# A planner that assumes one transfer rate at the start and a lower one after, with a smaller margin behind weight blocks

## The chip, the cores and the metric

The kernel runs on one core of one Trainium2 chip. The metric is the device time of one launch in microseconds (us). Each time below is the median of several runs, or the time of the one profiled execution where this is said.

## The reference, cut to what matters

One decoder layer on 512 tokens of width 2048, in float32. All weights are read from the chip's memory once per launch.

```python
mod = silu(c) @ w_ada + b_ada                 # 2048 -> 6 x 2048: sh1, sc1, g1, sh2, sc2, g2
h   = rms_norm(x, norm1_g) * (1 + sc1) + sh1
u   = h @ w_in                                # 512 x 2048 @ 2048 x 5656, split in groups
y_conv = short_conv_mixer(u_b, u_c, u_h)      # 1024 channels
k_cmp  = compress(k, cmp_w1_k, cmp_w2_k)      # and v_cmp: a small MLP over blocks of 32 tokens
y_attn = nsa_attention(q, k_cmp, v_cmp, k_slc, v_slc, k_win, v_win, gates)   # 8 heads x 128
x   = x + g1 * (concat(norm(y_conv), norm(y_attn)) @ w_out)
h   = rms_norm(x, norm2_g) * (1 + sc2) + sh2
x   = x + g2 * (relu(h @ w_ff1) ** 2 @ w_ff2) # 2048 -> 8192 -> 2048
out = rms_norm(x, normf_g)
```

## The kernel before, in words

The program has three parts, one after the other: the projections (everything up to the last column of `u`, some 0 to 557 us), attention with the first half of `w_out` (to about 745 us), and the rest of `w_out` with the feed-forward network (to the end). Each part is first only recorded: an object of class `Order` takes down every instruction with its engine, an assumed cost, and what it depends on. `Order.emit` then plans the part several times (`passes`), keeps the shortest plan, and issues the instructions in the planned order. Each engine, and the queue of transfers on SyncE (SP), then runs its own list strictly in that order on the chip. What an instruction waits for is set by its data; what stands ahead of it on its engine is set by the plan.

In `Order.plan` a transfer is priced by `rate`: it takes the wire for size over rate, one transfer after another, and the next one may be planned no earlier than 2 us before the wire is free. 512 KB take 1.28 us at 410 GB/s and 1.54 us at 340 GB/s. Of all instructions that could go next, the one that can start earliest is taken; ties go to the one that is wanted first (`late`). `x.slack` is added to the moment from which a transfer may start: the loads of the modulation matrix wait `SLACK` us behind the moment when their buffer is free, so that a block of weights that becomes ready in that time is planned ahead of them.

What is loaded in the projections, all in pieces of 512 KB:

- 16 blocks each of `w_kv`, `w_cv`, 32 of `w_conv`, 16 of `w_q`, 8 of `w_v`, 16 of `cmp_w1` (the compress MLP). Each lands in one of three buffers `raw`. ScalarE (ACT) copies it to the high part, VectorE (DVE) subtracts that to get the low part (rows `wh<-raw`, and `sw<-raw` for `cmp_w1`), and TensorE (PE) multiplies. The subtraction frees the `raw` buffer. `wh` has two pairs, so ACT can copy a block only when PE is done with the block two before. A block of `w_kv`, `w_cv`, `w_conv`, `w_q` gives PE 24 matmuls of 512 columns, a block of `cmp_w1` only 12 of 256 columns.
- 192 pieces of `w_ada`, the modulation matrix, into a ring `wa` of eight buffers, later four. For each one DVE does one dot product (`t<-wa,cs`; the results go to `acc` or `late`), which frees the buffer. The first third (sh1, sc1) is needed for the tokens `h` and has no slack or a slack of its own; the rest (g1, sc2, sh2, g2) is needed only after the projections. These are the late modulation loads.

At the end of the projections SP loads the first blocks of `w_oc` (`w_out` for the convolution half), DVE finishes the last heads (`q`), the mixed rows (`mix`) and the last dot products, sums the modulation (`mod<-late`), and attention begins: PE computes scores `s<-kslc,q` into three score buffers, DVE turns each into `p` and `pc`, and only then can PE fill the buffer again. DVE's first attention instruction is the memset of `pc`. Between scores, PE has matmuls `pw<-mix,wh` of `w_oc` to do.

All instructions recorded through `Order` carry one line of the source in the profile (L123), so rows are told apart by their tiles.

Of the kernel before, what the change touches and what calls it, by code (L numbers as in the profile page):

```python
# [35 lines left out]
NMAIN = 29  # L36
NSIDE = 7
NWA = 8
NBANK = 6
SLACK = 4.0  # L40
SOON = 10.0
BEHIND = 11.0

# [6 lines left out]
class Order:  # L50
# [2 lines left out]

    class Node:
        __slots__ = ("i", "eng", "call", "cost", "lag", "size", "preds", "succs", "late", "loose", "born",
                     "begin", "ready", "left", "lane", "slack", "due")

    def __init__(self, tc, tag, count, passes=1, pace=0.000456, rate=340e3):  # L60
        self.tc, self.tag, self.count, self.passes = tc, tag, count, passes
        self.lane, self.kept, self.slack, self.wide, self.pace = 0, set(), 0.0, (0.11, 0.00182), pace
        self.rate = rate
        self.nodes, self.past, self.seen, self.rings = [], {}, {}, {}
        self.outer, self.loose, self.due = set(), False, 0.0
        for e in ("tensor", "vector", "scalar", "sync", "gpsimd"):
            setattr(self, e, Order.Engine(self, e, getattr(tc.nc, e)))
# [132 lines left out]
    def plan(self, ideal, t, fixed):  # L200
        nodes = self.nodes
        ends = {}
        for name, by in self.seen.items():
            for i in set(by):
                ends.setdefault(i, []).append(name)
        users = {name: len(set(v)) for name, v in self.seen.items()}
        mine = sorted((n for x in nodes for n in x.born), key=lambda n: int(n.rsplit("_", 1)[1]))
        rank = {n: k for k, n in enumerate(mine)}

        for x in reversed(nodes):  # L210
            move = x.cost + x.lag if not x.size else 2.5 + x.size / self.rate
            x.late = min([nodes[s].late - (move if nodes[s].eng != "tensor" or x.eng != "tensor" else x.cost)
                          for s in x.succs] + [ideal.get(x.i, t + 10.0 - x.due)])

        free = dict.fromkeys(("tensor", "vector", "scalar", "sync", "gpsimd"), 0.0)
        wire = 0.0
        ready = {e: [] for e in free}
        lanes = {}
        for i in fixed or [x.i for x in nodes if x.eng == "tensor" and not x.loose]:
            lanes.setdefault(0 if fixed else nodes[i].lane, []).append(i)  # L220
        for lane in lanes.values():
            lane.reverse()
        slots = sorted([0.0] * (self.count - len(self.outer)))
        given = []
        while slots and len(given) < len(mine):
            given.append(slots.pop(0))
        for x in nodes:
            x.left, x.ready = len(x.preds), 0.0
            if not x.left and (x.eng != "tensor" or x.loose):
                ready[x.eng].append(x)  # L230
        out = []
        while len(out) < len(nodes):
            best = None
            for e in free:
                c = [(x, 0, None) for x in ready[e]]
                if e == "tensor":
                    c = [(x, -1, None) for x in ready[e]]
                    c += [(nodes[q[-1]], k, q) for k, q in lanes.items() if q and not nodes[q[-1]].left]
                for x, k, q in c:
                    at = max(free[e], x.ready + x.slack, wire - 2.0 if x.size else 0.0)  # L240
                    if x.born:
                        last = max(rank[n] for n in x.born)
                        if last >= len(given):
                            continue
                        at = max(at, given[last])
                    key = (at, k, x.late, x.i)
                    if best is None or key < best[0]:
                        best = key, x, q
            (at, *_), x, q = best
            e = x.eng  # L250
            if q is not None:
                q.pop()
            else:
                ready[e].remove(x)
            x.begin = at
            free[e] = at + x.cost
            end = at + x.cost + x.lag
            if x.size:
                wire = max(wire, at + 1.5) + x.size / self.rate
                end = wire + 0.7  # L260
            for n in ends.get(x.i, ()):
                users[n] -= 1
                if not users[n] and (n in rank or n in self.outer) and n not in self.kept:
                    if len(given) < len(mine):
                        given.append(max([end] + given[-1:]))
            for s in x.succs:
                y = nodes[s]
                y.left -= 1
                y.ready = max(y.ready, free[e] if e == y.eng == "tensor" else end)
                if not y.left and (y.eng != "tensor" or y.loose):  # L270
                    ready[y.eng].append(y)
            out.append(x)
        return max(free.values()), out
# [3 lines left out]
def hybrid_layer(ctx: ExitStack, tc: tile.TileContext, a, out):  # L277
    nc = tc.nc
# [13 lines left out]
    def pair(dtype=F32, name="m"):  # L292
        return slot(dtype, name)[:, :2 * T].rearrange("p (a b) -> p a b", a=2)
# [22 lines left out]
        tc.keep_in_program_order(filler(nc.tensor))  # L316

    xs = [pair(name="x2") for _ in range(NK // 2)]
    nc = order = Order(tc, xs[0].tensor.tag, NMAIN, passes=6, pace=0.000444, rate=410e3)
    order.wide = (0.24, 0.0021)  # L320
    ts = [small.tile([P, T], F32, name="t", tag="t", bufs=5) for _ in range(5)]
    scr, temps = ts[0].bitcast(BF16), cycle(ts[1:])
# [18 lines left out]
    class lane:  # L341

        def __init__(self, n):
            self.n = n
# [95 lines left out]
    def ada_steps(n):  # L440

        acc = halves_of(n)
        for i in range(2):
            w = ring[turn[0] % (4 if 0 in part_done else NWA)]
            turn[0] += 1
            order.slack = SLACK if n // NK not in (M_SC1, M_SH1) else 0.0 if n % NK else BEHIND
            nc.sync.dma_start(out=w, in_=a["w_ada"][2 * n + i])
# [275 lines left out]
    def more_ada(n):  # L723
        for _ in range(min(n, len(todo))):
            m = todo.pop(0)
            acc = halves_of(m)
            for i in range(2):
                w = ring[turn[0] % 4]
                turn[0] += 1
                order.slack = SLACK  # L730
                nc.sync.dma_start(out=w, in_=a["w_ada"][2 * m + i])
# [235 lines left out]
    nc = tc.nc  # L967
    temps = cycle(ts)
    nc = order = Order(tc, mix[0].tensor.tag, NMAIN, passes=6)
# [148 lines left out]
    nc = order = Order(tc, x1[0].tensor.tag, NMAIN, pace=0.000444)  # L1118
# [530 lines left out]
```

## Time and profile before

| what | value |
|---|---|
| median of 3 runs (lowest to highest) | 2099.62 us (2099.16 to 2104.02) |
| the profiled execution: time, span | 2096.75 us, 2095.0 us |
| mean granted TensorE clock | 0.991 |
| busy share of the span: PE, DVE, ACT, POOL | 98%, 90%, 48%, 6% |
| read from memory, written to it | 383.53 MB, 68.16 MB |

The span is the time from the first to the last instruction; the execution's own time has 1.75 us around it. In the profile a matmul's end is modelled, so a PE that is shown busy can still run below its peak; a row in which PE sat idle, with what ended the idle time, is firmer. A wait is put down to the last of the things waited for. "Granted clock" is the share of TensorE's full clock that it was given.

### The profile page before, as it was taken

What the parts mean: (1) busy time and instruction counts of PE and PEld (TensorE: products, weight loads), DVE (VectorE), ACT (ScalarE), POOL (GpSimd) and SP (SyncE); (2) the same over time, 40 slices, a digit from 0 to 9 for tenths busy, and PEclk for the clock granted to TensorE, in tenths of its full rate; (3) what the DMA queues carried; (4) which work ended last, traced back from release to release, by engine and by line L of the source; (5) the groups of instructions that cost most, each with busy time, mean ns of one, the idle gap of its engine ahead of it and who ended that gap; (6) DMA issues with size and microseconds to landing.
All of it is one profiled execution on the core that took longest, in us unless ns stands there. A gap on an engine that the chain in (4) does not pass through costs nothing.

```text
span 2095.0 us, 38213 instructions
## 1 busy us (share of the span) xinstructions
PE 2054.9 (98%) x15038; PEld 1920.0 (92%) x15038; DVE 1885.9 (90%) x3104; ACT 1007.7 (48%) x1465; POOL 128.1 (6%) x244
## 2 busy tenths in 40 slices
PE   9999999999999999999999999999999999999997
PEld 7888787898788779999999999999999999999997
DVE  7999997887898657999999999999999999999998
ACT  4432333232465435776666666666443333333355
POOL 0000000000000001022211121222000000000000
PEclk8999999999999999999999999999999999999999
DMA  8986488888511134476766666668975466476452
GB/s 343 348 325 231 174 294 324 311 292 307 200 63 69 62 134 152 136 227 207 211 210 205 208 214 198 213 206 285 347 274 211 163 248 227 138 254 239 144 181 99
DMA packets 144276, 454.19 MB, mean 217 GB/s; under 512 B 15840, under 2 KB 20320, under 8 KB 144096
## 3 DMA queue, kind: packets, MB, share of 16 engines
q1 hardware_dynamic: 108960, 386.72, 52.7%
q0 software_dynamic: 34048, 63.98, 10.1%
q8 instruction: 118, 1.93, 0.4%
q10 hardware_dynamic: 1088, 1.05, 0.1%
q14 instruction: 62, 0.51, 0.1%
HBM read 383.53 MB, written 68.16 MB: 216 GB/s over the span
## 4 chain that ended last, share of the span: by engine, by line
PE 90%; DVE 4%; DMA 3%; ACT 1%; issue 1%; SPq 0%; DVEq 0%; ACTq 0%
PE pf L123 63%; PE ps L123 19%; PE pw L123 4%; PE pv L123 2%; PE s L123 2%; DMA wa<-in_w_ada 1%; PE pt L123 1%; DMA raw<-in_cmp_w 1%; DVE wh L123 1%; DVE t L123 1%; DMA raw<-in_w_conv 0%; DMA x<-in_xt 0%; DVE x L123 0%; ACT wh L123 0%; DVE vz L123 0%
## 5 line engine op out<-in xcount | busy, mean ns | idle before, releaser
L123 PE MATMUL pf<-tk,hl 128*128 128x256 f32 x10704 | 1218.7, 276 | 0.5 <-ACT t L123 0.5
L123 PEld LDWEIGHTS pf<-tk,hl 128*128 128x128 f32 x10704 | 1217.1, 188 | 0.8 <-ACT t L123 0.7
L123 ACT ACTIVATE hl<-rw 128x1024 fp32r<-128x1024 f32 x269 | 285.7, 1063 | 338.3 <-PE pf L123 291.0
L123 DVE TENSOR_TENSOR hl<-rw,hl 128x1024 fp32r<-128x1024 f32 (+2 forms) x351 | 336.4, 968 | 32.4 <-ACT hl L123 31.9
L123 ACT ACTIVATE hl<-sg 128x1024 fp32r<-128x1024 f32 x180 | 191.1, 1062 | 217.3 <-PE pf L123 170.0
L123 DVE SCALAR_TENSOR_TENSOR t<-wa,cs 128x1024 bf16<-128x1024 f32 x190 | 231.7, 1220 | 30.7 <-DMA wa<-in_w_ada 29.0
L123 PE MATMUL ps<-h_m,wh 128*128 128x512 f32 x1080 | 252.3, 390 | 0.9 <-DVE h_m L123 0.9
L123 PEld LDWEIGHTS ps<-h_m,wh 128*128 128x128 f32 x1080 | 201.1, 188 | 42.4 <-DVE h_m L123 1.3
L123 ACT ACTIVATE wh<-raw 128x1024 fp32r<-128x1024 f32 (+1 forms) x106 | 112.7, 1064 | 257.3 <-PE ps L123 214.8
L123 DVE TENSOR_TENSOR hl<-sg,hl 128x1024 fp32r<-128x1024 f32 (+2 forms) x193 | 188.2, 986 | 27.1 <-ACT hl L123 26.9
L123 PE MATMUL ps<-h,wh 128*128 128x512 f32 x840 | 198.9, 395 | 2.9 <-ACT h L123 2.9
L123 PEld LDWEIGHTS ps<-h,wh 128*128 128x128 f32 x840 | 159.5, 191 | 36.7 <-ACT h L123 3.5
L123 DVE TENSOR_TENSOR wh<-raw,wh 128x1024 fp32r<-128x1024 f32 (+1 forms) x106 | 129.7, 1224 | 21.8 <-ACT wh L123 21.1
L123 DVE TENSOR_TENSOR sg<-sg,rw 128x1024 f32<-128x1024 f32 x120 | 145.8, 1215 | 0.0
L123 DVE SCALAR_TENSOR_TENSOR x<-pf,mod,x 128x256 f32<-128x256 f32 (+1 forms) x280 | 130.0, 483 | 13.5 <-PE pf L123 11.6
L123 POOL DMA_DIRECT2D g<-gt x192 | 101.1, 532 | 424.3 <-ACT hl L123 185.7
L123 PE MATMUL pw<-mix,wh 128*128 128x512 f32 x384 | 110.7, 407 | 0.0
L123 ACT ACTIVATE t<-t 128x512 f32<-128x512 f32 (+3 forms) x131 | 74.8, 571 | 15.9 <-DVE t L123 13.8
L123 DVE TENSOR_TENSOR sg<-rw 128x1024 f32<-128x1024 f32 x60 | 73.1, 1219 | 7.9 <-DMA rw<-in_w_f 4.8
L123 PEld LDWEIGHTS pw<-mix,wh 128*128 128x128 f32 x384 | 69.2, 190 | 10.8 <-issue 0.5
L123 DVE TENSOR_TENSOR rw<-rw 128x1024 f32<-128x1024 f32 x60 | 72.9, 1215 | 0.0
L123 ACT ACTIVATE gt<-t 128x512 fp32r<-128x512 f32 x96 | 60.3, 629 | 18.1 <-DVE t L123 15.2
(217 smaller groups left out, 1775.6 us busy)
## 6 DMA issues: line engine op xcount, KB each, us to landing
rw<-in_w_f SPq DMA_DIRECT2D x263, 512.0 KB, 4.2
wa<-in_w_ada SPq DMA_DIRECT2D x192, 512.0 KB, 6.0
tk<-g SPq DMA_DIRECT2D x114, 512.0 KB, 6.6
g<-gt POOLq DMA_DIRECT2D x192, 256.0 KB, 5.3
raw<-in_w_conv SPq DMA_DIRECT2D x32, 512.0 KB, 4.0
x<-in_xt SPq DMA_DIRECT2D x16, 512.0 KB, 5.7
raw<-in_w_kv SPq DMA_DIRECT2D x16, 512.0 KB, 5.5
raw<-in_w_cv SPq DMA_DIRECT2D x16, 512.0 KB, 5.1
```

Source lines behind the costliest of these rows:

```text
L123: x.i, x.eng, x.call = len(self.nodes), eng, (lambda: real(*args, **kw))
```

## The change

The first part's planner no longer takes 410 GB/s throughout. It takes 410 GB/s for transfers that begin before 40 us of planned time, and 340 GB/s for all later ones, also where it works back from when data is wanted (`late`). The two other planners took 340 GB/s before and still do. `SLACK` goes from 4 us to 1 us.

```diff
-SLACK = 4.0
+SLACK = 1.0
...
 class Order:
+    RATE, RUSH = 340e3, 410e3
...
-    def __init__(self, tc, tag, count, passes=1, pace=0.000456, rate=340e3):
+    def __init__(self, tc, tag, count, passes=1, pace=0.000456, rush=0.0):
...
-        self.rate = rate
+        self.rush = rush
...
-            move = x.cost + x.lag if not x.size else 2.5 + x.size / self.rate
+            move = x.cost + x.lag if not x.size else 2.5 + x.size / Order.RATE
...
             if x.size:
-                wire = max(wire, at + 1.5) + x.size / self.rate
+                wire = max(wire, at + 1.5)
+                wire += x.size / (Order.RUSH if wire < self.rush else Order.RATE)
                 end = wire + 0.7
...
-    nc = order = Order(tc, xs[0].tensor.tag, NMAIN, passes=6, pace=0.000444, rate=410e3)
+    nc = order = Order(tc, xs[0].tensor.tag, NMAIN, passes=6, pace=0.000444, rush=40.0)
```

No instruction is added or removed; the lists are permuted, in the projections only. POOL's list is the same. On SP the list is the same up to the seventh block of weights, on PE everything up to the first compress matmul. Two source lines were added, so L123 is L125 in the changed kernel. Three places:

First, the end of the projections on DVE. `wh<-raw` are subtractions (the last one is that of the first `w_oc` block), `t,late<-wa,cs` dot products, `MEMSET pc` is the first instruction of attention. Before:

```order
L123 TENSOR_TENSOR wh<-raw,wh 128x1024
L123 SCALAR_TENSOR_TENSOR q<-t,q 128x512
L123 TENSOR_TENSOR mix<-y,mix 128x512 x5
L123 TENSOR_TENSOR wh<-raw,wh 128x1024
L123 TENSOR_TENSOR mix<-y,mix 128x512 x3
L123 SCALAR_TENSOR_TENSOR t,late<-wa,cs 128x1024 x2
L123 TENSOR_TENSOR wh<-raw,wh 128x1024
L123 SCALAR_TENSOR_TENSOR t,late<-wa,cs 128x1024 x5
L123 TENSOR_TENSOR mod<-late 128x16
L123 TENSOR_TENSOR mod<-mod,vec 128x16
L123 MEMSET pc 128x96 x2
```

The same place on DVE in the changed kernel:

```order
L125 TENSOR_TENSOR wh<-raw,wh 128x1024
L125 SCALAR_TENSOR_TENSOR q<-t,q 128x512
L125 TENSOR_TENSOR mix<-y,mix 128x512 x6
L125 TENSOR_TENSOR wh<-raw,wh 128x1024
L125 SCALAR_TENSOR_TENSOR t,late<-wa,cs 128x1024 x3
L125 TENSOR_TENSOR wh<-raw,wh 128x1024
L125 SCALAR_TENSOR_TENSOR t,late<-wa,cs 128x1024
L125 TENSOR_TENSOR mod<-late 128x16
L125 TENSOR_TENSOR mod<-mod,vec 128x16
L125 TENSOR_TENSOR wh<-raw,wh 128x1024
L125 MEMSET pc 128x96 x2
```

Seven dot products stood behind the last `mix` rows, five of them behind the last subtraction; now four stand there, and all of them ahead of the last subtraction.

Second, the same place in SP's list of transfers, before:

```order
L123 DMA raw<-in_w_q 128x1024
L123 DMA wa<-in_w_ada 128x1024 x3
L123 DMA raw<-in_w_q 128x1024
L123 DMA wa<-in_w_ada 128x1024 x2
L123 DMA raw<-in_w_q 128x1024
L123 DMA wa<-in_w_ada 128x1024 x2
L123 DMA raw<-in_w_q 128x1024
L123 DMA wa<-in_w_ada 128x1024 x2
L123 DMA raw<-in_w_oc 128x1024
L123 DMA wa<-in_w_ada 128x1024 x4
L123 DMA raw<-in_w_oc 128x1024 x2
```

SP in the changed kernel, from the same `w_q` block (the thirteenth) on:

```order
L125 DMA raw<-in_w_q 128x1024
L125 DMA wa<-in_w_ada 128x1024 x3
L125 DMA raw<-in_w_q 128x1024
L125 DMA wa<-in_w_ada 128x1024
L125 DMA raw<-in_w_q 128x1024 x2
L125 DMA raw<-in_w_oc 128x1024 x3
```

The last six modulation loads stood behind the last `w_q` block, four of them behind the first `w_oc` block; now all 192 are ahead of the last two `w_q` blocks.

Third, the compress blocks in SP's list, from the third block of `cmp_w1` to the sixth, before:

```order
L123 DMA raw<-in_cmp_w 128x1024
L123 DMA raw<-in_w_conv 128x1024
L123 DMA wa<-in_w_ada 128x1024 x2
L123 DMA raw<-in_w_conv 128x1024
L123 DMA wa<-in_w_ada 128x1024
L123 DMA raw<-in_cmp_w 128x1024
L123 DMA wa<-in_w_ada 128x1024 x2
L123 DMA raw<-in_cmp_w 128x1024
L123 DMA wa<-in_w_ada 128x1024 x3
L123 DMA raw<-in_cmp_w 128x1024
```

The same stretch of SP's list in the changed kernel:

```order
L125 DMA raw<-in_cmp_w 128x1024
L125 DMA raw<-in_w_conv 128x1024
L125 DMA wa<-in_w_ada 128x1024 x2
L125 DMA raw<-in_cmp_w 128x1024
L125 DMA raw<-in_w_conv 128x1024
L125 DMA wa<-in_w_ada 128x1024 x2
L125 DMA raw<-in_cmp_w 128x1024
L125 DMA wa<-in_w_ada 128x1024 x3
L125 DMA raw<-in_cmp_w 128x1024
```

Between these two ends stood eight `wa` and two `w_conv`; now seven `wa` and two `w_conv` stand there, and the `wa` sit in other gaps.

Two counts over the whole lists: between the subtraction of the first `w_v` block and that of the eleventh `w_q` block DVE had 42 dot products and has 47 now. Between the first and the sixteenth compress block SP had 73 transfers and has 74 now; of the sixteen, the ninth, thirteenth and fourteenth stand two, two and three transfers further back in SP's list while PE uses them at the same place in its list, five matmuls and eight matmuls earlier.

## The prediction, before the run

> **What bounds the kernel now.** I read the page first, then the stretches, then the waits of PE. Its top and the shares of the chain that ended last:
>
> ```profile
> span 2095.0 us, 38213 instructions
> PE 2054.9 (98%) x15038; PEld 1920.0 (92%) x15038; DVE 1885.9 (90%) x3104; ACT 1007.7 (48%) x1465; POOL 128.1 (6%) x244
> PE 90%; DVE 4%; DMA 3%; ACT 1%; issue 1%; SPq 0%; DVEq 0%; ACTq 0%
> ```
>
> PE is the bound; 10% of the chain is other engines. The change permutes the projections only, so only PE's idle time there, and what it causes, can be won. The busy time by stretch (columns: PE, its weight loads, DVE, ACT, POOL, granted clock, DMA share, GB/s):
>
> ```profile
> 0.00:45.00 45.00, 39.98 (x166) 30.99 (x167) 33.05 (x57) 20.79 (x28) 0.20 (x4) 0.81 0.96 376
> 45.00:205.00 160.00, 159.07 (x702) 131.44 (x701) 152.21 (x262) 58.59 (x72) 0.00 (x0) 1.00 0.82 299
> 205.00:375.00 170.00, 162.79 (x802) 133.57 (x801) 148.11 (x208) 61.45 (x71) 0.00 (x0) 1.00 0.73 265
> 375.00:540.00 165.00, 162.94 (x898) 142.21 (x897) 136.38 (x217) 44.78 (x65) 0.00 (x0) 1.00 0.85 299
> 540.00:558.00 18.00, 18.00 (x86) 15.07 (x85) 17.89 (x27) 9.39 (x15) 0.00 (x0) 1.00 0.36 124
> 558.00:564.00 6.00, 0.83 (x4) 0.39 (x3) 4.31 (x15) 0.34 (x2) 0.00 (x0) 0.70 1.01 387
> 564.00:571.00 7.00, 7.00 (x29) 6.52 (x30) 3.61 (x25) 4.13 (x17) 0.00 (x0) 0.52 0.24 97
> 571.00:735.00 164.00, 164.00 (x864) 133.01 (x864) 135.26 (x389) 90.11 (x227) 0.00 (x0) 1.00 0.21 68
> ```
>
> PE's idle time is 5.0 us at the start, 0.9 in 45 to 205, 7.2 in 205 to 375 (where the compress blocks come in), 2.1 in 375 to 540, and 5.2 in the six microseconds in which the projections give way to attention. There the clock also falls, to 0.52 over the next seven. Behind it, to 735, PE is shown busy throughout: what PE gains at 564 it keeps. The wire is full only at the start (376 GB/s) and at the seam (387); in between it carries 265 to 299. All waits of PE from 205 to the seam (total, times, longest):
>
> ```profile
> PE ps L123 <- ACT sw L123: 6.3, 7, 1.6
> PE ps L123 <- DVE vv L123: 1.4, 1, 1.4
> PE ps L123 <- DVE sw L123: 0.7, 1, 0.7
> PE ps L123 <- DVE t L123: 0.6, 1, 0.6
> ```
>
> Compress blocks (`sw`) make 7.0 of these 9.0 us. Ordinary blocks make none.
>
> **The seam, step by step.** PE, SP and DVE in order of time there:
>
> ```profile
> 556.74 1.13 PE L123 MATMUL s<-kslc,q 128*128 128x160 f32 x9
> 557.71 0.91 PE L123 MATMUL pw<-mix,wh 128*128 128x512 f32 x3
> 563.79 0.93 PE L123 MATMUL s<-kslc,q 128*128 128x160 f32 x3 [5.17 <-DVE pc L123]
> ...
> 570.87 0.38 PE L123 MATMUL s<-kslc,q 128*128 128x288 f32 x1
> 541.46 14.52 SPq L123 DMA_DIRECT2D wa<-in_w_ada  x4
> 553.26 1.22 DVE L123 TENSOR_TENSOR wh<-raw,wh 128x1024 fp32r<-128x1024 f32 x1
> 554.39 1.22 DVE L123 SCALAR_TENSOR_TENSOR t<-wa,cs 128x1024 bf16<-128x1024 f32 x1
> 561.01 1.22 DVE L123 SCALAR_TENSOR_TENSOR t<-wa,cs 128x1024 bf16<-128x1024 f32 x1 [1.59 <-DMA wa<-in_w_ada]
> 562.63 0.25 DVE L123 MEMSET pc<- 128x96 f32 x2
> ```
>
> PE fills three score buffers, does three `pw`, and then stands 5.17 us until DVE has read a score. DVE could not: behind its last subtraction (553.26) it had five dot products, the last of which waited 1.59 us for its load, then the sums; the memset of `pc` came at 562.63. The load was late because SP spent 14.52 us on the last four, each behind the dot product that frees its buffer of the ring.
>
> *Term 1, the wait.* In the new lists all loads of `w_ada` are issued ahead of the last two `w_q` blocks, and the memset of `pc` stands directly behind the last subtraction. That one's time is set by PE, which frees `wh`: 553.26 + 1.22 gives `pc` at about 554.5, eight microseconds earlier and two before PE's first score. Even if DVE came 3 us late it would be there before PE is done with its three `pw` (558.62). Between the last `mix` and `pc` DVE had seven dot products and one subtraction, and has four and three: 3 x 1.3 us less, 2 x 1.22 us more, and the subtractions keep PE's pace. The whole 5.2 us go. Ends: 0 (DVE late by more than 5 us) and -5.2. I take -5.2. What is late next is DVE's own work on each score, 0.28 us and two short reads, which the `pw` cover.
>
> *Term 2, the clock.*
>
> ```profile
> 560.00:561.00 1.00, 0.00 (x0) 0.00 (x0) 0.00 (x0) 0.00 (x0) 0.00 (x0) 0.71 0.99 389
> 570.00:571.00 1.00, 1.00 (x7) 1.00 (x7) 0.08 (x1) 0.00 (x0) 0.00 (x0) 0.67 0.00 0
> ```
>
> 0.71 of one microsecond puts the fall to half at 560.4, 1.8 us after PE went idle; 0.67 puts the return at 570.7, 6.9 us after it resumed. PE ran 563.8 to 570.7 at half clock: at most 6.9 / 2 = 3.45 us are lost, and nothing if DVE sets the pace there. DVE is busy 3.61 of 7 us, so it is mostly PE: I take -2.8, ends 0 and -3.45. [...]
>
> **The compress blocks.** One of the waits, from its cause on:
>
> ```profile
> 249.43 0.33 SPq L123 DMA_DIRECT2D raw<-in_cmp_w  x1
> 254.88 1.22 DVE L123 SCALAR_TENSOR_TENSOR t<-wa,cs 128x1024 bf16<-128x1024 f32 x1 [1.87 <-DMA wa<-in_w_ada]
> 256.11 1.06 ACT L123 ACTIVATE sw<-raw 128x1024 fp32r<-128x1024 f32 x1 [1.99 <-DMA raw<-in_cmp_w]
> 257.21 0.33 PE L123 MATMUL ps<-sw,chi 128*66 128x256 f32 x1 [1.48 <-ACT sw L123]
> ...
> raw<-in_cmp_w SPq DMA_DIRECT2D x16, 512.0 KB, 5.1
> wa<-in_w_ada SPq DMA_DIRECT2D x192, 512.0 KB, 6.0
> ```
>
> Issued at 249.43, landed at 256.1, copied, and PE had waited. From issue to landing these take a median of 5.1 and the loads 6.0 us; at 410 GB/s the plan counts 1.5 + 1.28 + 0.7 = 3.5 us for a lone one, at 340 it counts 3.7. Both are optimistic, the new one 0.3 us less so per transfer and more where they queue.
>
> *Term 3.* For a gain speaks that the wire carried 265 GB/s there, under the new rate. For a loss: three compress blocks stand two or three transfers further back while PE wants them no later. The stretch has 74 transfers where it had 73, so the total load is the same. Both kinds of change act on single blocks, in both directions. Ends: -7.0 (all of those waits gone) and +7.0 (as much again). I take 0, midway, since the nearest row, the sum of the waits, is bound to either side alike.
>
> **The rows ahead of 205 us and the other moved rows.** SP's list is the same up to the seventh weight block, and between 45 and 205 PE loses 0.9 us. What covers a permutation there is that ACT waits for PE, not for data:
>
> ```profile
> ACT wh L123 <- PE ps L123: 214.8, 60, 5.9
> ```
>
> An ordinary block sits in its buffer until PE frees a `wh`. I cost this at nothing. Cover gone, each block would cost PE what it comes late.
>
> *Term 4, more dot products per block later on.* From the first `w_v` to the eleventh `w_q` block (412 to 520 us) DVE has 47 dot products instead of 42, 5 x 1.3 = 6.5 us more. The stretch, and what DVE waited for in it:
>
> ```profile
> 412.00:520.00 108.00, 105.94 (x642) 95.19 (x641) 85.99 (x140) 29.76 (x44) 0.00 (x0) 1.00 0.85 300
> DVE t L123 <- DMA wa<-in_w_ada: 14.9, 13, 3.0
> DVE wh L123 <- ACT wh L123: 6.3, 7, 1.9
> ```
>
> 86.0 busy plus 21.2 of waits is 107.2 of 108 us. With 92.5 busy, 15.5 us are left for waits. If the waits stay at 21.2, DVE and the subtractions behind its waits come late by 21.2 - 15.5 = 5.7 us. But a DVE that runs later finds more loads landed, and the loads themselves stand earlier. A ring of four needs 6.0 + 1.3 + 0.4 (issue) = 7.7 us for four dot products, 1.9 each, where 108 / 47 = 2.3 us are to be had. Ends: 0 and +5.7. I take +1.0, nearer to the row of the ring, which does not bind.
>
> **Sum.** -5.2 - 2.8 + 0 + 1.0 = -7.0 us on the profiled execution's 2096.75, 2089.75. The median of the runs is 2099.62, 2.9 us above that execution; forecast 2099.62 - 7.0 = 2092.6, 0.33% faster. About 0.3%, 6.3 us, is what a measurement of this kernel can tell from no change, so this is a forecast near that line.
>
> **The rivals.**
>
> *Larger gain.* The plan, nearer to what the wire gives, also clears the compress waits, and term 4 is nothing: -5.2 - 2.8 - 7.0 = -15.0, 2084.6. For it: 265 and 299 GB/s measured against 340 planned. Against: the latency is still planned two microseconds short, and those blocks did not move forward in SP's list. [...]
>
> *No change.* The gain at the seam is paid back by DVE in the `w_v` and `w_q` blocks: term 4 at its end, +5.7, gives -2.3 and 2097.3. It comes about where the ring's waits do not shrink when DVE is fuller: 13 waits for `wa` there say that the ring is close. For it also: a change that fixes little else. Against: the ring's 1.9 us per dot product.
>
> *Slower.* One mechanism: compress blocks that come so late that PE idles over 1.8 us, and the clock halves in mid-stage. Two or three transfers at 524288 bytes / 299 GB/s = 1.75 us are 3.5 to 5.3 us; the ninth, thirteenth and fourteenth block are the candidates. Each such wait costs about 4 us and 3.45 at half clock, 7.5. One leaves a small gain, two give -7.0 + 15 = +8, 2107.6: it decides from the second on. Against it: SP there waits on buffers more than on bytes (DMA share 0.73), so places in the list cost less than a transfer each. [...]
>
> **How the numbers follow.** The likeliest case, seam repaired and the rest about even, gets 0.52, with a range of its own of 2088 to 2098 and so three fifths of it faster by over 0.3% (0.31) and the rest within (0.21). Larger gain 0.15, all faster. No change 0.19. Slower 0.14. That makes 0.46 faster, 0.40 the same, 0.14 slower. The range takes in the larger gain to its figure and the no-change case with the spread of the runs, and leaves out the slower case: 2084.5 to 2101.
>
> **What would show it.** Term 1: no idle row of PE over 1 us between the last `w_q` matmul and the twelfth score; the memset of `pc` within 1 us of the last subtraction. Term 2: a granted clock of 1.00 from 540 to 735. Term 3: the sum of PE's waits for `sw` between 0 and 14 us, and no dip of the clock. Term 4: PE's idle time in the `w_v` and `w_q` blocks under 3 us. The forecast is wrong if `pc` is still late (DVE behind by over 4 us at the last `wh`), or if a compress wait passes 1.8 us and halves the clock.

## The result, and the profile after

The changed kernel takes 2080.81 us (median of 5 runs, 2080.06 to 2082.51), the kernel before 2099.42 us on the same chip (5 runs, 2096.21 to 2104.02). The ratio is 0.9912, 95% interval 0.9898 to 0.9925: 0.88% faster, where 0.33% was forecast, and outside the range. The profiled executions, 2082.51 and 2096.75 us, lie 14.2 us apart, the medians 18.6. On another chip the unchanged files gave 2083.01 against 2097.69, 14.7 apart (e7 below).

The head of the page after, and its busy time by stretch, in the columns of the prediction:

```profile
span 2080.7 us, 38230 instructions
PE 2051.0 (99%) x15038; PEld 1917.6 (92%) x15038; DVE 1885.8 (91%) x3104; ACT 1007.1 (48%) x1465; POOL 128.4 (6%) x244
```

```profile
45.00:205.00 160.00, 160.00 (x706) 132.21 (x705) 152.74 (x264) 58.96 (x73) 0.00 (x0) 1.00 0.83 301
205.00:375.00 170.00, 165.65 (x816) 135.96 (x815) 151.88 (x216) 62.30 (x74) 0.00 (x0) 1.00 0.78 274
375.00:540.00 165.00, 164.38 (x905) 143.85 (x904) 147.74 (x233) 49.06 (x71) 0.00 (x0) 1.00 0.86 307
540.00:558.00 18.00, 18.00 (x99) 15.60 (x98) 11.51 (x46) 9.12 (x24) 0.00 (x0) 1.00 0.38 131
558.00:564.00 6.00, 6.00 (x34) 5.14 (x34) 5.61 (x26) 3.50 (x12) 0.00 (x0) 1.00 0.28 87
564.00:571.00 7.00, 7.00 (x42) 6.09 (x40) 6.54 (x22) 5.38 (x17) 0.00 (x0) 1.00 0.00 0
```

From 540 to 571 PE has no idle time, and its clock is 1.00. From 205 to 540 it idles 5.0 us instead of 9.3, and from 45 to 205 none instead of 0.9. PE's waits from 205 to 545 are now:

```profile
PE ps L125 <- DVE sw L125: 1.9, 3, 1.5
PE ps L125 <- ACT sw L125: 1.5, 4, 0.7
PE ps L125 <- DVE t L125: 0.8, 1, 0.8
PE ps L125 <- DVE vv L125: 0.5, 1, 0.5
```

Compress blocks make 3.4 us (7.0 before), all waits 4.7 (9.0). The handover to attention, in order of time:

```profile
542.74 1.22 DVE L125 SCALAR_TENSOR_TENSOR t<-wa,cs 128x1024 bf16<-128x1024 f32 x1
...
547.04 1.23 DVE L125 TENSOR_TENSOR wh<-raw,wh 128x1024 fp32r<-128x1024 f32 x1 [2.65 <-ACT wh L125]
548.23 0.25 DVE L125 MEMSET pc<- 128x96 f32 x2
...
551.41 1.13 PE L125 MATMUL s<-kslc,q 128*128 128x160 f32 x9
...
553.12 0.46 PE L125 MATMUL s<-kslc,q 128*128 128x160 f32 x3
```

The last dot product begins at 542.74, the memset of `pc` follows the last subtraction at 548.23, three microseconds ahead of the first score, and the second group of scores (553.12) waits for nothing.

Two distances tell where the time went. From PE's first score to the first matmul of the third part (first `pf`) the profile has 191.8 us before (556.74 to 748.56) and 183.2 after (551.41 to 734.62): -8.6. The first score itself comes 5.3 earlier. From the first `pf` to the end it is 1346.4 and 1346.1.

### The profile page after: what moved, and what is told of

It is laid out like the page before. It is cut to its first block, busy times and chain, and to the rows that moved or that the text cites. A ratio compares the mean times of both kernels' runs of the same rounds, so it can differ in the third digit from the quotient of the medians.

```text
span 2080.7 us, 38230 instructions
## 1 busy us (share of the span) xinstructions
PE 2051.0 (99%) x15038; PEld 1917.6 (92%) x15038; DVE 1885.8 (91%) x3104; ACT 1007.1 (48%) x1465; POOL 128.4 (6%) x244
## 4 chain that ended last, share of the span: by engine, by line
PE 91%; DVE 4%; DMA 3%; ACT 1%; issue 1%; SPq 0%; DVEq 0%; ACTq 0%
PE pf L125 64%; PE ps L125 19%; PE pw L125 4%; PE pv L125 2%; PE s L125 2%; PE pt L125 1%; DMA raw<-in_cmp_w 1%; DMA wa<-in_w_ada 1%; DVE wh L125 1%; DMA raw<-in_w_conv 1%; DVE t L125 1%; DMA x<-in_xt 0%; ACT wh L125 0%; DVE x L125 0%; DVE vz L125 0%
## 5 line engine op out<-in xcount | busy, mean ns | idle before, releaser
L125 PE MATMUL pf<-tk,hl 128*128 128x256 f32 x10704 | 1218.7, 276 | 0.5 <-ACT t L125 0.5
L125 PEld LDWEIGHTS pf<-tk,hl 128*128 128x128 f32 x10704 | 1217.1, 188 | 0.8 <-ACT t L125 0.7
L125 ACT ACTIVATE hl<-rw 128x1024 fp32r<-128x1024 f32 x269 | 285.6, 1063 | 339.0 <-PE pf L125 285.3
L125 DVE TENSOR_TENSOR hl<-rw,hl 128x1024 fp32r<-128x1024 f32 (+2 forms) x351 | 336.3, 967 | 32.4 <-ACT hl L125 32.0
L125 ACT ACTIVATE hl<-sg 128x1024 fp32r<-128x1024 f32 x180 | 191.1, 1062 | 219.5 <-PE pf L125 165.4
L125 PE MATMUL ps<-h_m,wh 128*128 128x512 f32 x1080 | 252.1, 390 | 0.0
L125 DVE SCALAR_TENSOR_TENSOR t<-wa,cs 128x1024 bf16<-128x1024 f32 x190 | 231.6, 1219 | 14.0 <-DMA wa<-in_w_ada 12.2
L125 PEld LDWEIGHTS ps<-h_m,wh 128*128 128x128 f32 x1080 | 201.0, 188 | 41.6 <-DVE h_m L125 0.4
L125 ACT ACTIVATE wh<-raw 128x1024 fp32r<-128x1024 f32 (+1 forms) x106 | 112.8, 1064 | 255.5 <-PE ps L125 226.7
L125 DVE TENSOR_TENSOR hl<-sg,hl 128x1024 fp32r<-128x1024 f32 (+2 forms) x193 | 188.2, 985 | 25.1 <-ACT hl L125 24.9
L125 PE MATMUL ps<-h,wh 128*128 128x512 f32 x840 | 198.8, 394 | 2.9 <-ACT h L125 2.9
L125 PEld LDWEIGHTS ps<-h,wh 128*128 128x128 f32 x840 | 159.0, 190 | 36.7 <-ACT h L125 3.5
L125 DVE TENSOR_TENSOR wh<-raw,wh 128x1024 fp32r<-128x1024 f32 (+1 forms) x106 | 129.8, 1225 | 23.3 <-ACT wh L125 22.6
L125 DVE TENSOR_TENSOR sg<-sg,rw 128x1024 f32<-128x1024 f32 x120 | 145.8, 1215 | 0.0
L125 DVE SCALAR_TENSOR_TENSOR x<-pf,mod,x 128x256 f32<-128x256 f32 (+1 forms) x280 | 129.8, 484 | 13.7 <-PE pf L125 11.8
L125 POOL DMA_DIRECT2D g<-gt x192 | 101.4, 533 | 425.0 <-issue 188.0
L125 PE MATMUL pw<-mix,wh 128*128 128x512 f32 x384 | 109.4, 404 | 0.0
L125 ACT ACTIVATE t<-t 128x512 f32<-128x512 f32 (+3 forms) x131 | 74.7, 571 | 15.6 <-DVE t L125 13.6
L125 DVE TENSOR_TENSOR sg<-rw 128x1024 f32<-128x1024 f32 x60 | 73.1, 1218 | 8.4 <-DMA rw<-in_w_f 6.0
L125 PEld LDWEIGHTS pw<-mix,wh 128*128 128x128 f32 x384 | 68.5, 189 | 10.7 <-issue 0.5
L125 DVE TENSOR_TENSOR rw<-rw 128x1024 f32<-128x1024 f32 x60 | 72.8, 1214 | 0.0
L125 ACT ACTIVATE gt<-t 128x512 fp32r<-128x512 f32 x96 | 60.2, 629 | 15.7 <-DVE t L125 13.4
```

The source lines that it names most:

```text
L125: x.i, x.eng, x.call = len(self.nodes), eng, (lambda: real(*args, **kw))
```

## The experiments

Sixteen experiments were run, e1 to e16 (e7 is the changed kernel once more). The table gives them in the words used below: the ratio to the kernel before on the same chip; the wait of PE at the handover ("seam"); the distance from first score to first `pf`; all waits of PE from 205 to 545; and of these the ones at compress blocks (`sw`). The medians are of 4 to 12 runs; the last four columns are each from one profiled execution of that kernel.

| kernel | median | ratio (95% interval) | seam wait | score to `pf` | waits 205 to 545 | of these at compress blocks |
|---|---|---|---|---|---|---|
| before | 2099.42 | 1 | 5.2 | 191.8 | 9.0 | 7.0 |
| changed | 2080.81 | 0.9912 (0.9898 to 0.9925) | none | 183.2 | 4.7 | 3.4 |
| e1, rate alone | 2098.16 | 1.0001 (0.9990 to 1.0012) | 11.0 | 198.1 | 3.7 | 3.2 |
| e2, margin alone | 2086.40 | 0.9949 (0.9936 to 0.9963) | none | 183.5 | 4.0 | 2.4 |
| e3, 340 from the start | 2083.22 | 0.9931 (0.9917 to 0.9945) | none | 183.2 | 3.5 | 2.7 |
| e4, before with PE kept busy | 2095.71 | 0.9987 (0.9976 to 0.9997) | 1.8 | 185.7 | 11.7 | 7.8 |
| e5, before, margin 7 | 2129.45 | 1.0144 (1.0126 to 1.0163) | 29.6 | 216.3 | 13.6 | 12.0 |
| e6, before, 375 GB/s | 2099.73 | 1.0008 (0.9998 to 1.0019) | 8.1 | 193.5 | 5.7 | 4.1 |
| e7, changed again | 2083.01 | 0.9929 (0.9917 to 0.9942) | none | 183.3 | 3.1 | 1.5 |
| e8, later landing | 2087.57 | 0.9947 (0.9935 to 0.9959) | none | 183.2 | 7.5 | 4.5 |
| e9, changed, 300 GB/s | 2106.73 | 1.0043 (1.0030 to 1.0056) | 9.5 | 204.6 | 4.2 | 1.1 |
| e10, changed, margin 0 | 2083.70 | 0.9928 (0.9916 to 0.9941) | none | 183.1 | 3.1 | 1.8 |
| e11, changed, margin 2 | 2084.76 | 0.9934 (0.9921 to 0.9946) | none | 183.2 | 4.4 | 2.8 |
| e12, one matmul ahead of the feed-forward | 2085.09 | 0.9934 (0.9920 to 0.9947) | none | 183.2 | 4.1 | 2.2 |
| e13, before, 12 loads uncoupled | 2099.32 | 0.9996 (0.9985 to 1.0008) | 4.4 | 191.7 | 8.5 | 6.5 |
| e14, changed, 12 loads uncoupled | 2082.06 | 0.9915 (0.9902 to 0.9927) | none | 183.2 | 3.4 | 2.4 |
| e15, before, loads uncoupled | 2092.64 | 0.9969 (0.9959 to 0.9979) | 2.8 | 191.3 | 5.4 | 4.9 |
| e16, changed, loads uncoupled | 2081.30 | 0.9913 (0.9899 to 0.9928) | none | 183.2 | 3.3 | 2.0 |

### Which half does it: e1, e2, e3, e7

e1 is the changed kernel with the old margin, e2 the kernel before with the new one, e3 the changed kernel without the first 40 us at 410 GB/s, e7 the changed kernel once more.

```diff
# e1, to the changed kernel
-SLACK = 1.0
+SLACK = 4.0
# e2, to the kernel before
-SLACK = 4.0
+SLACK = 1.0
# e3, to the changed kernel
-pace=0.000444, rush=40.0)
+pace=0.000444, rush=0.0)
```

> The changed kernel with SLACK back at 4 us, so the two rates alone. In its lists ten modulation loads stand behind the last w_q block, eight of them behind the first w_oc block, and seven dot products behind the last subtraction (before: six, four and five). Theory A (the rates ease the waits for compress blocks, the margin repairs the seam): the projections end some 4 us earlier than before (552 to 553 us), but PE's wait at the seam grows from 5.2 to 8 to 12 us and the clock halves again, so the time is 2099 to 2104 us, not faster than before. Theory B (the margin eases both): the projections end at 556 to 558 us, the seam is as bad as under A, time 2102 to 2108 us. Theory C (the rates do all of it): no wait at the seam, time near 2081 us.

> The kernel before with SLACK at 1 us, so the smaller margin alone, at 410 GB/s throughout. In its lists no modulation load stands behind the last seven w_q blocks and no dot product behind the last mix rows. Theory A: no wait of PE over 1 us at the seam and a granted clock of 1.00 there, -8 to -9 us; waits for compress blocks as before (6 to 8 us) or larger, because loads go ahead of compress blocks; projections end at 556 to 559 us; time 2090 to 2093 us. Theory B: projections end at 551 to 552 us, time 2081 to 2085 us. Theory C: the seam as before, time 2097 to 2101 us.

> The changed kernel with 340 GB/s from the first transfer on (rush=0). The seam's lists are like the changed kernel's, so no wait there under any theory. If the 410 GB/s of the first 40 us matter, PE idles more before 45 us (changed kernel: 5.5 us) and the time is 1 to 5 us above the changed kernel's 2080.8; if not, it is within 1.5 us of it (2079 to 2082.5).

> The changed kernel once more, for a second profile and for runs on one chip with the others. If its gain of 18.6 us over the kernel before holds where the profiles differ by 14.3 us, it comes out at 2079 to 2082 us beside a kernel before at 2098 to 2100; if part of the gain was chance between runs, at 2082 to 2086.

The margin alone gives 0.51% and repairs the seam whole (183.5). Its time, 2086.40, lies between the ranges of theories A and B: the seam came as A says, but the waits in 205 to 545 fell to 4.0 us, where A left them at 6 to 8. The rate alone gives nothing: it takes the waits in 205 to 545 down to 3.7 us, the first score comes at 548.33, 8.4 us earlier than before, and the seam gives it back:

```profile
563.09 0.93 PE L125 MATMUL s<-kslc,q 128*128 128x160 f32 x3 [11.02 <-DVE pc L125]
```

Scores begin at 548.33, and the second group waits 11.02 us for `pc`, which still stands behind the dot products. So the waits in the projections fall with either half, and the falls do not add (3.7 and 4.0 us alone, 4.7 and 3.1 together). The smaller margin is what repairs the seam; the lower rate alone made it worse. e3 and e7 differ by 0.2 us: the first 40 us at 410 GB/s made no difference that these runs tell. e7's time is in the range that its expectation left to chance between runs, so the gain is 15 to 19 us by these two comparisons. e7 also shows what a profile's detail varies by: 3.1 us of waits in 205 to 545 where the first run had 4.7. With the lists of before, three profiles have 9.0, 8.5 (e13) and 11.7 (e4).

### How much of each: e5, e6, e9, e10, e11

The same two numbers, moved past their values in both directions:

```diff
# e5, to the kernel before
-SLACK = 4.0
+SLACK = 7.0
# e6, to the kernel before
-passes=6, pace=0.000444, rate=410e3)
+passes=6, pace=0.000444, rate=375e3)
# e9, to the changed kernel: 300 GB/s in place of 340, in the first planner alone
+        self.rate = 300e3 if rush else Order.RATE
...
-                wire += x.size / (Order.RUSH if wire < self.rush else Order.RATE)
+                wire += x.size / (Order.RUSH if wire < self.rush else self.rate)
# e10 and e11, to the changed kernel
-SLACK = 1.0
+SLACK = 0.0   # e11: 2.0
```

> The kernel before with SLACK at 7 us instead of 4, still 410 GB/s: the margin alone, in the other direction. In its lists 18 dot products stand behind the last subtraction (before: five) and ten modulation loads behind the last w_q block. If the margin sets how far the late loads fall behind, and so the wait at the seam: 18 dot products at 1.3 us (data there) to 1.9 us (ring of four) from 554.4 us put pc at 578 to 588 us, so PE waits 19 to 30 us there instead of 5.2, and the time is 2112 to 2124 us. PE's waits between 205 us and the seam (before: 9.0 us): if the margin sets them too they grow to 10 us or more; if they differ from plan to plan without order they may come out anywhere from 3 to 10 us.

> The kernel before at 375 GB/s throughout, midway between its 410 and the changed kernel's 340, with SLACK still 4 us. Seven dot products and six loads behind the last subtraction and block, so the wait at the seam is 9 to 12 us as in the run with the rates alone (11.0), under any theory. Theory P (the slower the plan takes transfers to be, the fewer waits): PE's waits between 205 us and the seam lie between the 9.0 us of before and the 3.7 us of the rates alone, 5 to 8 us, DVE's waits for loads between 27 and 16 us; time 2098 to 2102 us. Theory L (the waits differ from plan to plan without order, and the plan before was a poor draw): they come out near 4 us or at 9 us and more.

> The changed kernel with 300 GB/s in place of 340 for the later part of the first plan; everything else as changed. Theory R (the lower rate itself brings the loads earlier to the dot products and so takes the matmuls' waits away; the seam only hears the margin): waits of the matmuls in 205-545 at or under the changed kernel's 3 to 5 us, the seam without a wait as at 340 GB/s with margin 1, time 2079 to 2084. Theory O (what counts is where the written-out order leaves the last loads and dot products, whichever number moved them): at 300 GB/s six wa loads stand behind the first w_oc block again and six dot products behind the last subtraction, so the wait before the first score returns with 8 to 11 us (rate alone, with as many loads behind, gave 11.0), the clock is halved there for 10 to 14 us, and the stretch from the first score's beginning to the FFN's first matmul takes 196 to 199 us in place of 183.2: 2091 to 2098.

> The changed kernel with the margin at 0 us in place of 1. All wa loads stand ahead of the last three w_q blocks. Theory M (a smaller margin is better until the weight blocks come too late): seam clean, 183.2 us from first score to FFN as with margin 1, and the matmuls' waits in 205-545 at 3 to 5 us: 2080 to 2084. Rival (loads let in ahead of blocks now make blocks land late): waits of matmuls or ScalarE for blocks grow to 7 us or more, 2086 to 2090.

> The changed kernel with the margin at 2 us in place of 1. Two wa loads stand behind the first w_oc block. If the seam's wait grows evenly with the margin (at 410 GB/s: 1 none, 4 5.2 us, 7 29.6 us), 0 to 2 us of it come back, under the 1.8 us of idleness after which the clock was halved before: 183 to 185.5 us from first score to FFN, time 2081 to 2086. If it is a step (the first load behind the w_oc block brings it), the wait is 4 us or more with half the clock for 10 us, 190 us to the FFN, and 2088 to 2092.

At margin 7 the wait at the seam is 29.57 us, in the expected range; the time, 2129.45, is above its range, since the projections too became longer (first score at 562.96, 6.2 us later than before). Its row for the scores, and its largest row of waits in 205 to 545:

```profile
595.68 0.93 PE L123 MATMUL s<-kslc,q 128*128 128x160 f32 x3 [29.57 <-DVE pc L123]
```

```profile
PE ps L123 <- ACT sw L123: 11.7, 9, 3.3
```

Margins of 0, 1 and 2 in the changed kernel all leave the seam clean, and their times lie within 4 us. At margin 2 two loads do stand behind the first `w_oc` block again, but their dot products stay ahead of the last subtraction. What decides is how many dot products stand between the last subtraction and `pc`: with none the seam has no wait; five make 5.2 us (before), six 9.5 (e9), seven 8.1 and 11.0 (e6, e1; in e1 PE began its first score 2.0 us ahead of the last subtraction, in e6 2.4 us behind it), eighteen 29.6 (e5). Margin 3 was not run, so where between 2 and 4 the wait comes in is open.

The rate alone, at margin 4, moves both places, in opposite directions: at 410, 375 and 340 GB/s (before, e6, e1) the waits in 205 to 545 are 9.0, 5.7 and 3.7 us, as theory P has it, and the wait at the seam is 5.2, 8.1 and 11.0 us. The times are the same within their intervals.

e9 is the sharpest miss of a simple story. A lower rate still, closer to what the wire carried in the trace before (265 to 299 GB/s), is slower than the kernel before (1.0043). Theory O named the place; the size it gave was too small (196 to 199 us from first score to `pf`, where it took 204.6, and half clock for 10 to 14 us, where it lasted 23.9), as PE also waited for ACT and for the last subtraction there. The seam of e9, PE and DVE apart:

```profile
558.40 1.22 PE L126 MATMUL pw<-mix,wh 128*128 128x512 f32 x2 [2.46 <-ACT qr L126]
561.24 0.80 PE L126 MATMUL pw<-mix,wh 128*128 128x512 f32 x1 [1.61 <-DVE wh L126]
571.55 0.93 PE L126 MATMUL s<-kslc,q 128*128 128x160 f32 x3 [9.52 <-DVE pc L126]
```

```profile
561.11 1.21 DVE L126 SCALAR_TENSOR_TENSOR t<-wa,cs 128x1024 bf16<-128x1024 f32 x1
...
568.78 1.23 DVE L126 SCALAR_TENSOR_TENSOR t<-wa,cs 128x1024 bf16<-128x1024 f32 x1 [0.29 <-DMA wa<-in_w_ada]
...
570.40 0.25 DVE L126 MEMSET pc<- 128x96 f32 x2
```

Six dot products, from 561.11 to 570.0, stand behind the last subtraction, of 1.2 us each and only 1.42 us of waits for loads. The waits in 205 to 545 are as small as in the changed kernel (4.2). A planned rate nearer to the measured one therefore does not by itself make the plan better; it moves loads, and where the last of them falls is decided by the whole plan.

### The clock at the handovers: e4, e12

e4 is the kernel before with five matmuls of no use ahead of the first score; e12 the changed kernel with one between attention and feed-forward. Their results are not read.

```diff
# e4; e12 has one, ahead of the first matmul of the feed-forward part
+    for _ in range(5):
+        tc.keep_in_program_order(tc.nc.tensor.matmul(turned[0], ones,
+            ones[:, None, :].to_broadcast([P, NQ, P]), start=True, stop=True))
```

> The kernel before with five extra matmuls (128x128 by 128x512 float32, about 0.86 us each at full clock) put on PE between the projections and the first score; their result is overwritten, nothing else moves. They fill most of the wait at the seam without shortening it: PE still cannot go on before DVE reaches pc at 562.6 us. If the half clock behind the wait costs what the prediction took (2.8 us, at most 3.45), the granted clock stays at 1.00 there and the time falls by 2 to 3.5 us to 2096 to 2097.5, although PE has 4.3 us more to do. If attention there is paced by DVE and ACT, or the extra matmuls only push the scores back, the time stays at 2099 to 2100 or rises by up to 1 us.

> The changed kernel with one matmul of no use (f32, 128x512, about 0.86 us at full clock) between attention and FFN, its result left unread in a buffer of PSUM. If the 3.4 us of half clock that some runs show there (731.9-735.3 in one, 747.9-751.3 in another) come from TensorE standing idle at this place, the stretch is at full clock and the kernel is up to 1.5 us faster, 2079 to 2083; if the idleness is elsewhere or chance, the matmul costs its own 0 to 0.9 us: 2081 to 2085. The clock of the stretch tells more than the time, which this can hardly move beyond its spread.

e4's PE and its clock at the seam:

```profile
558.24 4.45 PE L974 MATMUL pt<-ones 128*128 128x512 f32 x10
562.13 1.53 PE L123 MATMUL s<-kslc,q 128*128 128x160 f32 x9
...
566.16 0.56 PE L123 MATMUL s<-kslc,q 128*128 128x160 f32 x3 [1.77 <-DVE pc L123]
```

```profile
558.00:571.00 13.00, 11.23 (x59) 8.05 (x58) 10.38 (x45) 5.25 (x20) 0.00 (x0) 1.00 0.76 269
```

`pc` is as late as ever, but of the 5.17 us PE idles 1.77, and the clock stays at 1.00. From the end of the projections to the first `pf` the profile has 189.6 us (558.24 to 747.87) instead of 191.8, and in it 3.9 us of fill (558.24 to 562.13) for 3.4 us of idleness. So by these two profiles the half clock cost 2.2 + 0.5 = 2.7 us. The kernel with more work on its bounding engine is faster by 2.6 us (0.6 to 5.0 by the interval). e12 decides nothing: its time is that of the changed kernel's runs, and its clock from 740 to 760 was 0.91 where the changed kernel's was 1.00 without the matmul. Some runs have some 3.5 us at half clock near that place (e10: clock 0.77 from 730 to 735 and 0.88 from 735 to 740) and some not (changed: 1.00 from 715 to 760); the idleness of PE in the row ahead of the first `pf` is not shown to be the cause.

### Why the waits in the projections fell: e8, e13, e14, e15, e16

e8 plans every transfer of the first part to land 2 us later, so that dot products stand later behind their loads.

```diff
# e8, to the changed kernel
+        self.later = 2.0 if rush else 0.0
...
-            move = x.cost + x.lag if not x.size else 2.5 + x.size / Order.RATE
+            move = x.cost + x.lag if not x.size else 2.5 + self.later + x.size / Order.RATE
...
-                end = wire + 0.7
+                end = wire + 0.7 + self.later
```

> The changed kernel with 2 us more assumed between the end of a transfer on the wire and its landing, in the first part's planner only: 5.7 us for a lone transfer where the runs show medians of 5 to 6 us. Theory P: DVE's waits for loads between 205 us and the seam fall from 12.2 us to under 8, PE's waits from 4.7 to 2 to 4 us, no wait at the seam, time 2078 to 2081 us, 1 to 3 us under the changed kernel. Theory L: PE's waits anywhere from 3 to 9 us, time 2079 to 2087 us.

DVE's waits for loads in 205 to 545 are down to 1.4 (12.2 in the changed kernel). The heads of DVE's and of PE's waits there:

```profile
DVE wh L126 <- ACT wh L126: 23.9, 23, 2.7
DVE vv L126 <- ACT gates L126: 3.6, 2, 1.8
```

```profile
PE ps L126 <- DVE sw L126: 4.5, 3, 2.3
PE ps L126 <- DVE wh L126: 1.6, 1, 1.6
PE ps L126 <- ACT wh L126: 0.9, 1, 0.9
```

Yet PE waits 7.5 us, 6.1 of them for DVE's subtractions, and the time is above the ranges of both theories. Fewer waits of DVE are not in themselves fewer waits of PE.

e15 and e16 keep the orders of before and after and cut the coupling: the 128 late dot products read a tile that is there from the start, so none waits for a load and no load waits for a dot product. The loads still run; the four late parts of the modulation are left out of the result. (e13 and e14 were the same edit reaching only 12 of the 128; with ratios of 0.9996 and 0.9915, and waits of 8.5 and 3.4 us, they say no more than repeats of before and after.)

```diff
# e15 to the kernel before, e16 to the changed kernel; stand_in, left out here,
# puts a dot product of cs with cs in the place of the one recorded last
             dot(w, i, acc)
+            if n // NK in LATE:
+                stand_in(i, acc)
...
                 dot(w, i, acc)
+                if m // NK in LATE:
+                    stand_in(i, acc)
```

> The kernel before in its own order, with the dot products of g1, sc2, sh2, g2 reading a tile that is there from the start in place of the loaded pieces. The loads still run, at the same places of SP's list, but no dot product waits for one and no load waits for a dot product. (Left out: those four parts of the modulation don't hold w_ada's products.) Theory D (the matmuls' waits at compress blocks come from the coupling: DVE stands for a load, or SP stands for a dot product and issues the next block late): DVE's 27.4 us of waits for loads in 205-545 go, and the matmuls' waits there fall from 9.0 us to 2.5 or less (the waits for vv and t, 2.0, stay). At the seam DVE still has its five dot products behind the last subtraction, without the 1.59 us wait for the load: the memset of pc 1.6 us earlier, so a wait of 3.6 us is left there, and the half clock stays. Sum -6.5 - 1.6 = -8, 2090. Rival (blocks come late by themselves, from the wire or from the subtraction that frees their buffer): waits in 205-545 stay at 7 us or more, time 2094 to 2098.

> The same edit on the changed kernel, in its own order (the same parts of the modulation left out). Theory D: the matmuls' 4.7 us of waits in 205-545 fall to 2.5 or less, as in the kernel before, so that the two kernels differ in what is left at the seam alone; seam without a wait; 2078 to 2081. Rival: 4 to 5 us of waits stay, 2081 to 2083.

> The kernel before in its own order, with all 128 dot products of g1, sc2, sh2, g2 reading a tile that is there from the start (the run before this one had reached twelve of them). The loads run at the same places of SP's list; none of those dot products waits for a load and no load waits for one. (Left out: those four parts of the modulation don't hold w_ada's products.) Theory D (the matmuls' waits at compress blocks come from the coupling through the ring): DVE's 27.4 us of waits for loads in 205-545 go, and the matmuls' waits there fall from 9.0 us to 2.5 or less. At the seam DVE has its five dot products without the 1.59 us for the load: pc 1.6 us earlier, a wait of 3.6 us left, the half clock stays. Sum -6.5 - 1.6 = -8, 2090 to 2092. Rival (blocks come late by themselves, from the wire or from the subtraction that frees their buffer): waits in 205-545 stay at 7 us or more, time 2094 to 2099.

> The same edit, all 128 dot products, on the changed kernel in its own order (the same parts of the modulation left out). Theory D: the matmuls' 4.7 us of waits in 205-545 fall to 2.5 or less, seam without a wait, 2077 to 2081. Rival: 3 to 5 us of waits stay, as they do from run to run with the loads coupled, 2080 to 2083.

What is left of PE's waits in 205 to 545 in e15, and at compress blocks in e16:

```profile
PE ps L123 <- ACT sw L123: 4.9, 5, 2.0
PE ps L123 <- DVE vv L123: 0.5, 1, 0.5
```

```profile
PE ps L125 <- DVE sw L125: 1.6, 1, 1.6
PE ps L125 <- ACT sw L125: 0.4, 2, 0.3
```

The seam of e15 (`L416` marks the dot products that read the standing tile) and its clock there:

```profile
552.99 0.91 PE L123 MATMUL pw<-mix,wh 128*128 128x512 f32 x3
...
553.95 1.22 DVE L416 SCALAR_TENSOR_TENSOR t<-cs 128x1024 bf16<-128x1024 f32 x1
...
556.72 0.93 PE L123 MATMUL s<-kslc,q 128*128 128x160 f32 x3 [2.82 <-DVE pc L123]
```

```profile
556.00:557.00 1.00, 0.28 (x1) 0.28 (x2) 1.00 (x5) 0.40 (x2) 0.00 (x0) 0.85 0.03 8
566.00:567.00 1.00, 1.00 (x5) 0.91 (x4) 1.00 (x4) 0.75 (x4) 0.00 (x0) 0.53 0.00 0
```

The order of before loses 3.6 of its 9.0 us of waits without the coupling (5.4 stay) and 0.31% of its time; the changed order loses nothing that can be told (3.3 us, in the spread of 3.1 to 4.7 of its other runs). Neither theory had it whole: by these profiles the coupling of DVE and SP through the ring makes some 3.6 us of the 9.0, 2.1 of them at compress blocks, and about 2 us more go with the other order of the blocks. At the compress blocks themselves the order does more than the coupling: 4.9 us in e15 and 2.0 in e16. The wait that the prediction showed at 257.21 is of the second kind: it is in e15 too (257.59, 1.99 us) and not after. There the fourth compress block is issued at 248.1 and lands in 4.4 us; before, with one `w_conv` and one `wa` more between it and the third, it was issued at 249.43 and took 6.6.

At the seam e15 holds a second reading. The wait shrinks from 5.17 to 2.82 us, and the distance from first score to `pf` by only 0.5. By the rows the clock fell at 556.7 and came back at 566.9, 10.2 us, as long as before (560.4 to 570.7); but now PE works through all of it and loses up to 10.2 / 2 = 5.1 us where it lost up to 3.45. 2.82 + 5.1 = 7.9 stands against 5.17 + 3.45 = 8.6.

No experiment beats the changed kernel: margins 0 and 2 and e3 end within 4 us of its runs.

## Why the prediction was wrong

*Terms 1 and 2, the seam, were right.* -8.0 forecast, -8.6 measured from first score to first `pf`. The chain was as told: no load behind the last `w_q` blocks, `pc` 1.2 us after the last subtraction began, no wait, full clock. e2 shows that the margin alone does it, e5 that more margin does the reverse, and e4 puts the clock at 2.7 us against 2.8. Wait and clock then make 7.9 of the 8.6; where the other 0.7 us went no run tells. The two terms are not independent, though: e15 took half the wait away and kept nearly all of the cost.

*Term 3 failed.* "I take 0, midway, since the nearest row, the sum of the waits, is bound to either side alike." Compress blocks' waits went from 7.0 to 3.4 us: -3.6, half-way to the end of -7.0 (and to 1.5 in e7, the same kernel). The sum of the waits was not bound to either side alike: in all eight other plans with a lower rate or a smaller margin (e1, e2, e3, e6, e8 to e11) it is smaller than before, 1.1 to 4.5 us, and in the one with a larger margin (e5) it is 12.0. So the direction was not the chance of one plan. Why the order does it is shown only in part. e15 measured the coupling, DVE standing for loads and SP for dot products: without it the old order keeps 4.9 of its 7.0 us, so 2.1 hung on it. (Its two sides were not tried apart; SP stands longer behind dot products after than before, 69.6 us against 23.0, and the changed kernel does not pay for it.) The rest went with the places of single blocks, of which only the one at 257.21 was followed to its cause. The prediction quoted a wait of DVE for a load at 254.88 and used it only as a sign of late landing.

*Term 4 failed in sign.* +1.0 was taken, and the five further dot products cost PE nothing: from 412 to 520 it idles 0.6 us where it idled 2.1.

```profile
412.00:520.00 108.00, 107.38 (x650) 96.52 (x649) 94.59 (x155) 30.36 (x45) 0.00 (x0) 1.00 0.93 332
DVE t L125 <- DMA wa<-in_w_ada: 4.9, 10, 1.6
```

DVE is 8.6 us busier there (6.5 was counted), and its waits for loads fell from 14.9 to 4.9. In e15, without such waits, PE's waits in that stretch fell as well, from 2.0 to 0.5 us. That is the branch that the prediction named ("a DVE that runs later finds more loads landed") and did not take.

*The rows ahead of 205 us* were costed at nothing and gave 0.9: the one wait there, at 132.6, is gone.

Together: -8.6, -4.3 (all waits in 205 to 545) and -0.9 make -13.8 of the 14.2 us between the profiles. That is within 1.2 us of the rival "larger gain" (-15.0, with a chance of 0.15); the median, 2080.81, lies below its 2084.6. Its mechanism was only half right. About half of the compress waits went in this pair, and term 4 was nothing, as it says. But being "nearer to what the wire gives" is not the whole reason: the margin alone, at 410 GB/s, left 2.4 us of them (e2), and at 300 GB/s, where they are smallest (1.1 us, e9), the seam made the kernel slower than before.

*The offset from profile to median* added the rest of the miss. I carried 2.9 us from the profiled run of before to its median. The changed kernel's profiled run is at the upper end of its five, 1.7 above the median, so that 14.2 turned into 18.6; on the other chip it was 14.7. The runs of before spread over 2091.5 to 2105.4 (23 runs on one chip). Why single runs differ by several microseconds was not settled, but two places of it show. Ahead of 45 us the half clock lasted 17.0 to 17.1 us in some profiles (before, changed, e12) and 13.7 in others (e14, e16); with the changed kernel's lists the first score came at 551.4 and 550.4 in the former and at 548.2 to 548.7 in the latter and in e7. And from the first `pf` to the end, where the lists are the same, the profiles have 1346.1 to 1351.3 us. So the pair compared above shows the gain of the projections at its low end: 5.3 us to the first score, where e7 has 8.1.

The slower rival (a compress wait long enough to halve the clock) did not come in the changed kernel. It is not empty: e5 has compress waits of up to 3.3 us, and 0.98 of the clock from 205 to 375.

One sum of the prediction does not come out as written; the forecast does not hang on it. One slow compress wait gives -7.0 + 7.5 = +0.5 us and not "a small gain".

## What to carry to other kernels

Where PE idles at a handover, read what stands in the list of the engine it waits for, between its last urgent instruction and the one awaited. Each instruction there lengthens the wait (none: no wait, five: 5.2 us, eighteen: 29.6), and a planner's number that moves them away at one value may bring them back at the next (margin 1 cleared the place at 340 GB/s and not at 300). A sum of waits is not "bound to either side alike" because single blocks move both ways: one run with the number moved the other way (e5, 12.0 us for 7.0) would have told the direction. Shortening an idle stretch that still halves the clock saves little: in e15, 2.35 us less of idleness saved 0.5.

## What the runs showed of the hardware

The half clock lasted 10.2 us at the seam of before (560.4 to 570.7) and of e15 (556.7 to 566.9), 13.7 in e1 (553.3 to 567.0), 23.9 in e9 (557.3 to 581.2) and 30.7 in e5 (569.1 to 599.8). In these runs it fell 1.8 us after PE went idle (before), 2.8 (e15), 1.2 (e1), 1.3 (e9) and 3.0 (e5), and came back 6.9 us after PE resumed (before), 10.2 (e15), 3.9 (e1), 9.6 (e9, from the scores at 571.55) and 4.1 (e5). In e4 PE was idle for 1.77 us and the clock stayed at 1.00. In e9 PE was idle for 1.85 us up to 545.35, and some of what followed ran at half clock although PE was at work: the 22 matmuls from 546.61 took 6.88 us, where 22 from 538.20 took 5.30. The clock of 0.89 from 540 to 558 makes that an estimated 3.2 us (18 x 0.11 x 2, less the 0.7 us after 557.3). What sets these times no run tells.
